# Sixteen experts of a mixture-of-experts layer taken two at a time, one in each 64-column half of TensorE

## The chip, the core and the metric

The kernel runs on one core of one Trainium2 chip. The metric is the device time of one execution in microseconds; lower is better. TensorE (PE) multiplies, ScalarE (ACT) and VectorE (DVE) empty the accumulation banks (PSUM) and do elementwise work, GpSimd (POOL) adds and broadcasts, and SyncE (SP) issues the transfers (DMA).

## What is computed

One decoder layer over 256 tokens of 2048 channels. A token-mixing part gives x1; each token is then routed to 2 of 16 experts. An expert has two input matrices of 2048 x 1024 (gate, up) and one output matrix of 1024 x 2048 (down):

```python
def expert_block(args):
    xb, e = args
    hb = jax.nn.silu(xb @ w_gate[e]) * (xb @ w_up[e])
    return hb @ w_down[e]
...
x = _layer_norm(ALPHA * x + mix, ln1_g[i], ln1_b[i])
...
ple = jax.nn.sigmoid(x @ ple_w_gate[i]) * (p[i] @ ple_w_proj[i])
x = _layer_norm(ALPHA * x + ffn + ple, ln2_g[i], ln2_b[i])
```

`ffn` is the sum over a token's two experts, weighted by the router. All is float32.

## The kernel before, in words

SBUF holds 12 large buffers of 16 KB per partition (`B`, `NB = 12`). Most of them hold weights: `load_one` (L129) takes one buffer for one load of 2 MB, `prefetch` (L142) starts loads as long as buffers are free beside those in `state["reserve"]`, and `done` (L152) gives a buffer back after its last matmul and calls `prefetch`. All loads go over SP's queue in one fixed order (`spec`), and each waits there until the readers of the buffer that it takes are done. `keep(n)` sets buffers aside; `BR` turns one of them into a long-lived tile.

**First part** (token mixing, L226 to L520): every weight piece is split into two rounded parts (float32r, `hi` and `lo`), and three float32r products replace one float32 product.

**Expert part.** For each expert `e`, `gate_up` takes 8 loads: 16 chunks of 128 channels times two matrices times two 512-column pieces. The tokens of the expert (up to 64 slots, `CAP`) are the 64-column stationary operand, and the two 512-column pieces of one matrix run in the two 64-column halves of the array (`mm_gu`, L755, matmul L757). `hidden` (L760) makes silu(gate) * up out of the two banks, turns it by four transposes (L775) and copies it to SBUF before the down product may begin. `mm_d` (L780, matmul L783) then takes 4 loads. The result is copied out by ACT (`evac`, L789), and `combine` (L812) brings the slots back to the tokens: a float32 product with the weighted selection matrix `PT`, in eight products of 64 rows (L801), with eight DVE additions into `acc` (L810). This runs as `late` work inside the next expert's `hidden`.

Small work is put between the loads by a list `bg`, from which `pop_bg` takes one piece after each load: `gather` (L702, matmuls L708), which builds the tokens `xg` of the next pair of experts by a one-hot product; `spread` and `weighted` (L678, L686: the weighted selection matrices, transposes L696); `keep_T` (transposes of x1 for the gated embedding) and `residual`.

After each of experts 6 to 13 comes one block of the gated embedding, `ple` (L728): 8 short matmuls (L737) and 64 long ones (L742) on one load. Its second weight, `wp`, lies in a large buffer of its own. Long-lived in large buffers are x1, xg, `misc` (the selection matrices and the copied results), acc, from expert 4 on x1T, and from expert 6 on wp.

Before the last expert stands `overflow` (L925): a branch that runs only if an expert has over 64 tokens, and that every engine must pass (L927). The last expert's columns come in blocks of 256, 256, 256, 128 and 128 (`last_expert`, L854), with statistics (L898) after each; then follow the layer norm (L1040, L1045) and the eight stores (L1059).

Of the kernel before, what the change touches and what calls it, by code (L numbers as in the profile page):

```python
# [17 lines left out]
T = 256  # L18
# [8 lines left out]
SCALE = 128.0 ** -0.5  # L27
NB = 12
PLE0 = 6
# [3 lines left out]
def trunk(ctx, tc, I, out):  # L33
# [69 lines left out]

    xw, xd = I["exp_w"], I["exp_d_last"]

    def spec_ple(i):
        spec(("ple", i), [(slice(0, 4096), I["ple_w_gate"][i].rearrange("p c f -> p (c f)"))])

    def spec_exp(e):
        for i in range(8):  # L110
            spec(("gu", e, i), [(slice(0, 4096), xw[e, i])])
        for i in range(4):
            spec(("ed", e, i), [(slice(0, 4096), xw[e, 8 + i] if e < NE - 1 else xd[i])])

    for e in range(NE):
        spec_exp(e)
        if e == PLE0 - 1:
            spec(("wp", 0), [(None, I["ple_w_proj"].rearrange("(c p) d -> p c d", p=128), 2)])
        if 0 <= e - PLE0 < 8:
            spec_ple(e - PLE0)  # L120
# [7 lines left out]

    def load_one():  # L129
        key, parts = loads[state["next"]]  # L130
        t = B("w")
        for p in parts:
            if p[0] is None:
                d = t if len(p) == 3 else t[:, p[3]:p[3] + 8 * p[4]]
                SP.dma_start(d.rearrange("p (c f) -> p c f", c=p[2]), p[1])
            else:
                SP.dma_start(t[:, p[0]], p[1])  # L137
        tiles[key] = t
        state["next"] += 1
        state["out"] = state.get("out", 0) + 1  # L140
# [71 lines left out]
    slots = C("slots", [128, 2, 64])  # L212
    POOL.iota(slots, pattern=[[0, 2], [1, 64]], base=1, channel_multiplier=0, allow_small_or_imprecise_dtypes=True)
# [452 lines left out]
    grp = {}  # L666
    back = {}
    long = {}

    def onehot(g):  # L670
        P = S("P")[:, 0:256].rearrange("p (a e s) -> p a e s", a=2, e=2)
        es = slice(2 * g, 2 * g + 2)
        for a in range(2):
            DVE.tensor_tensor(P[:, a], slots[:, 0:1, :].to_broadcast([128, 2, CAP]),  # L674
                              pos[:, a, es, None].to_broadcast([128, 2, CAP]), op=OP.is_equal)
        grp[g] = (P.rearrange("p a e s -> p a (e s)"), xgs[:, g % 2])

    def spread(e):  # L678
        W = S("W").rearrange("p (a e k s) -> p a e k s", a=2, e=2, k=2)
        for k in range(2):  # L680
            for a in range(2):
                DVE.tensor_scalar(W[:, a, k], slots, pos[:, a, e + k:e + k + 1], wA[:, a, e + k:e + k + 1],
                                  op0=OP.is_equal, op1=OP.mult)
        back[e] = W

    def weighted(e):  # L686
        if not long.get("misc"):
            long["misc"] = BR("misc").rearrange("p (i f) -> p i f", i=8)
            long["pT"] = long["misc"][:, 7, :].rearrange("p (c t) -> p c t", c=2)
            SP.dma_start(long["pT"], I["pT"])  # L690
        W = back[e]
        PT = long["misc"][:, (e // 2) % 2, :]
        ps = AUX()
        for k in range(2):
            for a in range(2):
                PE.transpose(ps[:, k * T + a * 128:k * T + (a + 1) * 128],  # L696
                             W[:, a, k].rearrange("p k s -> p (k s)"), ident)
        ACT.activation(PT, ps, AF.Copy)
        back[e] = PT[:, 0:T]
        back[e + 1] = PT[:, T:2 * T]  # L700

    def gather(g, cp):  # L702
        P, xg = grp[g]
        ps = AUX()
        for j in range(2):
            c = 2 * cp + j
            for a in range(2):
# [5 lines left out]
                          op0=OP.mult, op1=OP.add)  # L713

# [13 lines left out]
    def ple(i):  # L728
        if i == 0:
            long["wp"] = take(("wp", 0)).rearrange("p (c d) -> p c d", c=2)  # L730
# [4 lines left out]
        for a in range(2):  # L735
            for c in range(2):
                PE.matmul(pw[:, a * 256:(a + 1) * 256], long["pT"][:, c, a * 128:(a + 1) * 128], long["wp"][:, c, cs],  # L737
                          start=(c == 0), stop=(c == 1))
# [10 lines left out]
        POOL.tensor_add(long["acc"][:, :, cs], long["acc"][:, :, cs], s.rearrange("p (a f) -> p a f", a=2))  # L749
        done()  # L750
        if i == 7:
            free(2)
# [7 lines left out]
    def hidden(pg, pu, late=None, fill=0):  # L760
        s = S("s")
        hT = S("hT")
        ps = AUX()
        for k in range(2):
# [3 lines left out]
            DVE.tensor_mul(s[:, ks], s[:, ks], pu[:, ks])  # L768
        while late:
            late.popleft()()  # L770
        if fill:
            busy(fill)
# [5 lines left out]
        return hT.rearrange("p (j k s) -> p j k s", j=4, k=2)  # L778

    def mm_d(py, hT, w, fc):  # L780
        for b in range(2):
            for hf in range(2):
# [29 lines left out]
    def combine(y, PT, first=False):  # L812
        for b in range(2):
            for a in range(2):
                combine_unit(y, PT, first, a, b)
# [304 lines left out]
```

## Time and profile before

| | |
|---|---|
| time, median of 3 runs | 1643.28 us (1642.66 to 1643.73) |
| the profiled execution, its own time | 1642.69 us |
| its span, first to last instruction | 1641.0 us |
| PE busy | 1595.6 us (97%) |
| DVE busy | 559.9 us (34%) |
| ACT busy | 400.0 us (24%) |
| moved by DMA | 540.10 MB, mean 329 GB/s |

The first part takes about the first 615 us, the expert part the rest. "Busy" of PE counts pipelined matmuls with modelled ends, so that a nearly full share does not say that the array works at its peak. The GB/s of the DMA are read by stretch: the largest value that any long stretch shows is the measure of a full stretch.

### The profile page before, as it was taken

How to read it: one execution, taken by the hardware profiler on the slowest of the kernel's cores; microseconds unless marked ns; L12 is line 12 of the kernel's file. 1: busy time of each engine (PE TensorE's matmuls, PEld its weight loads, DVE VectorE, ACT ScalarE, POOL GpSimd, SP SyncE). 2: the span in 40 equal slices, each digit the busy share in tenths (PEclk: the TensorE clock that was granted, in tenths of full speed). 3: DMA queues.
4: the chain of work that ended last, by engine and by line, in shares of the span. 5: the costliest groups of instructions: out<-in, count | busy, mean ns of one | idle time of the engine just before them, and what ended most of it. 6: DMA issues, size and time to landing. Idle time of an engine off the chain costs nothing. (4 is left out here: it accounts for less than half of the span.)

```text
span 1641.0 us, 18130 instructions
## 1 busy us (share of the span) xinstructions
PE 1595.6 (97%) x7558; PEld 941.1 (57%) x7558; DVE 559.9 (34%) x996; ACT 400.0 (24%) x700; POOL 40.0 (2%) x41
## 2 busy tenths in 40 slices
PE   8999999999999999999999999999999999999994
PEld 6888878888888874433333344453544535445323
DVE  6555675656556652122022211112011120111126
ACT  5555555454545441100001000000000000000001
POOL 0000000000000000000000000000000000000012
PEclk9999999999999999999999999999999999999997
DMA  9743544255557767999999999999998999999994
GB/s 387 330 154 137 182 181 192 116 205 185 182 198 292 295 242 298 394 397 427 427 427 426 427 425 427 426 424 428 389 427 374 379 428 374 426 382 373 427 384 170
DMA packets 42586, 540.10 MB, mean 329 GB/s; under 512 B 7042, under 2 KB 7042, under 8 KB 9602
## 3 DMA queue, kind: packets, MB, share of 16 engines
q1 hardware_dynamic: 42500, 538.90, 80.3%
q8 instruction: 60, 0.98, 0.2%
q14 instruction: 26, 0.21, 0.0%
HBM read 536.78 MB, written 2.10 MB: 328 GB/s over the span
## 5 line engine op out<-in xcount | busy, mean ns | idle before, releaser
L757 PE MATMUL mm<-w,xg 128*64 128x512 f32 x2048 | 461.3, 598 | 4.4 <-PEq L927 2.6
L283 PE MATMUL mm<-pc,xh 128*128 128x512 f32 x1152 | 362.8, 395 | 6.0 <-ACT pc L264 5.4
L265 DVE TENSOR_TENSOR pc<-w,pc 128x512 fp32r<-128x512 f32 x416 | 290.9, 710 | 198.9 <-ACT pc L264 196.3
L264 ACT ACTIVATE pc<-w 128x512 fp32r<-128x512 f32 x416 | 259.7, 630 | 233.4 <-DVE pc L265 179.8
L757 PEld LDWEIGHTS mm<-w,xg 128*64 128x64 f32 x2048 | 139.7, 137 | 265.8 <-issue 249.7
L283 PEld LDWEIGHTS mm<-pc,xh 128*128 128x128 f32 x1152 | 213.8, 189 | 51.2 <-ACT pc L264 5.9
L283 PE MATMUL mm<-pc,xl 128*128 128x512 f32 x576 | 225.4, 391 | 0.0
L783 PE MATMUL mm<-w,hT 128*64 128x512 f32 x960 | 211.3, 595 | 0.0
L783 PEld LDWEIGHTS mm<-w,hT 128*64 128x64 f32 x960 | 66.8, 137 | 127.2 <-issue 126.6
L712 DVE TENSOR_SCALAR xg<-aux,gc 128x128 f32<-128x128 f32 x64 | 26.2, 410 | 318.2 <-ACT xg L711 318.2
L283 PEld LDWEIGHTS mm<-pc,xl 128*128 128x128 f32 x576 | 108.5, 188 | 22.9
L742 PE MATMUL mm<-w,x1T 128*128 128x256 f32 x512 | 111.8, 379 | 0.0
L742 PEld LDWEIGHTS mm<-w,x1T 128*128 128x128 f32 x512 | 97.3, 190 | 13.2
L711 ACT ACTIVATE xg<-aux,gc 128x128 f32<-128x128 f32 x64 | 29.3, 458 | 287.0 <-PE aux L708 287.0
L708 PEld LDWEIGHTS aux<-P,x 128*128 128x128 f32 x512 | 61.9, 191 | 51.0 <-issue 50.3
L748 DVE TENSOR_TENSOR s<-s,aux 128x512 f32<-128x512 f32 x8 | 5.5, 688 | 238.5 <-ACT s L747 238.5
L283 PE MATMUL mm<-pc,mixh 128*128 128x512 f32 x256 | 79.0, 390 | 0.0
L801 PE MATMUL aux<-misc 64*128 64x512 f32 x240 | 73.4, 629 | 2.6 <-DVE acc L810 2.6
L708 PE MATMUL aux<-P,x 128*128 128x128 f32 x512 | 73.8, 287 | 0.7 <-DVE P L674 0.7
L810 DVE TENSOR_TENSOR acc<-acc,aux 128x512 f32<-128x512 f32 x112 | 68.4, 680 | 14.8 <-PE aux L801 14.8
L767 DVE TENSOR_TENSOR s<-s,mm 128x256 f32<-128x256 f32 x32 | 13.4, 418 | 160.3 <-ACT s L766 160.3
L794 ACT ACTIVATE misc<-mm 128x512 f32<-128x512 f32 x30 | 17.7, 597 | 182.4 <-PE mm L783 182.4
(197 smaller groups left out, 834.1 us busy)
## 6 DMA issues: line engine op xcount, KB each, us to landing
w<-in_exp_w_dram SPq DMA_DIRECT2D x188, 2048.0 KB, 14.1
w<-in_w_in_dram SPq DMA_DIRECT2D x34, 2048.0 KB, 8.5
w<-in_w_o_dram SPq DMA_DIRECT2D x8, 2048.0 KB, 8.2
w<-in_ple_w_gate_dram SPq DMA_DIRECT2D x8, 2048.0 KB, 14.1
w<-in_w_out_a_dram SPq DMA_DIRECT2D x4, 2048.0 KB, 8.2
w<-in_w_out_b_dram SPq DMA_DIRECT2D x4, 2048.0 KB, 8.4
w<-in_exp_d_last_dram SPq DMA_DIRECT2D x4, 2048.0 KB, 30.8
w<-in_w_in_dram SPq DMA_DIRECT2D x3, 1024.0 KB, 12.7
```

What stands on the lines that cost most here:

```text
L264: ACT.activation(hi, w, AF.Copy)
L265: DVE.tensor_sub(lo, w, hi.bitcast(F32))
L283: PE.matmul(ps[a], l[:, c, as_], r, start=(first and n == 0), stop=(last and n == 2))
L708: PE.matmul(ps[:, j * 128:(j + 1) * 128], x1[:, a, c * 128:(c + 1) * 128], P[:, a, :], start=(a == 0), stop=(a == 1))
L711: ACT.activation(xg[:, c, :], ps[:, 0:128], AF.Identity, scale=gc[:, 0, c:c + 1], bias=gc[:, 1, c:c + 1])
L712: DVE.tensor_scalar(xg[:, c + 1, :], ps[:, 128:256], gc[:, 0, c + 1:c + 2], gc[:, 1, c + 1:c + 2], op0=OP.mult, op1=OP.add)
L742: PE.matmul(ps[:, a * 256:(a + 1) * 256], x1T[:, c, a * 128:(a + 1) * 128], w[:, c, :], start=(c == 0 and a == 0), stop=(c == DC - 1), ski ...
L757: PE.matmul(ps[64 * hf:64 * hf + 64, :], x, w[:, hf * 512:(hf + 1) * 512], start=(c == 0), stop=(c == DC - 1), skip_group_check=True, tile ...
L783: PE.matmul(py[b][64 * hf:64 * hf + 64, :], hT[:, fc % 4, fc // 4, :], w[:, hf * 1024 + b * 512:hf * 1024 + b * 512 + 512], start=(fc == 0 ...
L794: ACT.activation(y[-1], p, AF.Copy)
L801: PE.matmul(ps, PT[64 * hf:64 * hf + 64, a * 128:(a + 1) * 128], y[b][64 * hf:64 * hf + 64, :], start=True, stop=True, tile_position=(64 * ...
L810: DVE.tensor_add(xb, xb, pss[hf])
```

## The change

Experts are taken in pairs. For a pair `g`, one 64-column half of TensorE holds the tokens of one expert, the other half those of the other, and each of the four 512-column products of a chunk is now two matmuls, one per expert, into one bank. The work of a pair is four products of two banks each: "A" and "B" (each half of the hidden channels, gate and up, 8 loads) and "0" and "1" (each half of the output columns, 4 loads). The weights lie in DRAM in that order. The turn of a product's hidden rows is not done between the products but after the fourth chunk of the next product ("A") or the third of it ("B"). The routing weight is multiplied in on the hidden rows (`wc`), so that the selection matrix holds only 0 and 1 (`PO`); the results are split into two rounded parts and go back to the tokens by 128-row float32r products of both experts at once (`scatter`), one after each chunk of the following product. Small work is taken after each chunk, that is twice per load. `misc` and `wp` no longer take large buffers; the embedding blocks (`PLE`) stand in pairs 1 to 6, twice in pairs 4 and 5. The overflow branch stands before the last pair. The last pair's last 1024 columns come in blocks of 512, 256, 128 and 128.

```diff
-PLE0 = 6
+
+PLE = [(1, "B"), (2, "B"), (3, "B"), (4, "B"), (4, "1"), (5, "B"), (5, "1"), (6, "B")]
...
+    Pm = C("Pm", [128, 2, 2, 128])
+    PO = C("PO", [128, 2, T], F32R)
+    wc = C("wc", [128, NP + 1])
+    hTs = [C(f"hT{k}", [128, 4, 128]) for k in range(2)]
+    pT = C("pT", [128, 2, T])
+    SP.dma_start(pT, I["pT"])
...
+    def selection(P, w, i, n):
         ps = AUX()
...
+        for a in range(2):
+            PE.transpose(ps[:, a * 128:(a + 1) * 128], P[:, a], ident)
+        for a in range(2):
+            PE.matmul(ps[:, 256:258], P[:, a], w[:, a, :], start=(a == 0), stop=(a == 1), skip_group_check=True)
+        ACT.activation(PO[:, i, :], ps[:, 0:T], AF.Copy)
...
     def mm_gu(ps, x, w, c):
-        for hf in range(2):
-            PE.matmul(ps[64 * hf:64 * hf + 64, :], x, w[:, hf * 512:(hf + 1) * 512],
-                      start=(c == 0), stop=(c == DC - 1), skip_group_check=True, tile_position=(0, 64 * hf))
...
+        for k in range(2):
+            for e in range(2):
+                es = slice(64 * e, 64 * e + 64)
+                PE.matmul(ps[k][es, :], x[:, es], w[:, e, k, :], start=(c == 0), stop=(c == DC - 1),
+                          skip_group_check=True, tile_position=(0, 64 * e))
...
+    def inner(ph, g, xg, at):
+        ps = [MM(), MM()]
+        for i in range(8):
+            w = take((ph, g, i)).rearrange("p (c e k f) -> p c e k f", c=2, e=2, k=2)
+            for j in range(2):
+                mm_gu(ps, xg[:, 2 * i + j, :], w[:, j], 2 * i + j)
+                if j:
+                    done()
+                step(at, 2 * i + j)
+        return ps
...
+    def hidden(ps, n):
+        pg, pu = ps
         s = S("s")
...
+            DVE.scalar_tensor_tensor(s[:, ks], s[:, ks], wc[:, n:n + 1], pu[:, ks], op0=OP.mult, op1=OP.mult)
+        return s
...
+    def evac(ps, n=512):
         y = []
...
+        for p in ps:
+            h, l = S("yh", F32R)[:, 0:n], S("yl", F32R)[:, 0:n]
+            ACT.activation(h, p[:, 0:n], AF.Copy)
+            DVE.tensor_sub(l, p[:, 0:n], h.bitcast(F32))
+            y.append((h, l))
         return y
...
+    def scatter(y, i, o, a, first=False, n=512, stat=None):
+        ps = AUX()
+        for j in range(2):
+            PE.matmul(ps[:, 0:n], PO[:, i, a * 128:(a + 1) * 128], y[j], start=(j == 0), stop=(j == 1))
+        xb = long["acc"][:, a, o:o + n]
+        if first:
+            DVE.tensor_copy(xb, ps[:, 0:n])
...
+            DVE.tensor_add(xb, xb, ps[:, 0:n])
+        if stat is not None:
+            DVE.bn_stats(fst[:, a, stat, :], xb)
...
+    keep(2)
+    onehot(Pm[:, 0], pair_of(pos, 0))
+    gather(Pm[:, 0], xgs[:, 0], 0)
+    gather(Pm[:, 0], xgs[:, 0], 1)
     weights()
...
+        if g == NP - 1:
+            for f in back:
+                f()
+            back = []
+            keep(-2)
+            overflow()
+        ps = inner("A", g, xg, events(back, 1))
...
+        s = hidden(ps, g)
+        ples(g, "A")
+        ps = inner("B", g, xg, {3: lambda: turn_hidden(s, hTs[0])})
+        s = hidden(ps, g)
+        ples(g, "B")
+        if g == 0:
+            long["acc"] = BR("acc").rearrange("p (a d) -> p a d", a=2)
+        ps = outer("0", g, {2: lambda: turn_hidden(s, hTs[1])})
...
+        y = evac(ps)
+        ples(g, "0")
+        at = events(scatters(y, i, 0, g == 0, 0 if g == NP - 1 else None), 1)
...
+        ps = outer("1", g, at)
+        drain()
+        back = scatters(evac(ps), i, 1024, g == 0)
+        ples(g, "1")
```

How this moves the instructions, at three places. On PE, between the end of one expert's input product and its down product, followed by an embedding block, there stood before (L757 input products, L801 the way back to the tokens, L775 turn, L783 down, L737 and L742 embedding):

```order
L757 MATMUL mm<-w,xg 64x512 x24
L801 MATMUL aux<-misc 128x512 x8
L775 MATMUL aux<-ident,s 128x128 x4
L783 MATMUL mm<-w,hT 64x512 x32
L737 MATMUL aux<-w,misc 128x256 x4
L742 MATMUL mm<-w,x1T 128x256 x32
L757 MATMUL mm<-w,xg 64x512 x8
L708 MATMUL aux<-P,x_3542 128x128 x4
L757 MATMUL mm<-w,xg 64x512 x8
```

Now, for a pair, from the end of product "A" on (L746 input products, L799 turn, L723 and L728 embedding, L753 down, L816 the way back):

```order
L746 MATMUL mm<-w,xg 64x512 x24
L799 MATMUL aux<-ident,s 128x128 x4
L746 MATMUL mm<-w,xg 64x512 x48
L723 MATMUL aux<-wpt,pT 128x256 x4
L728 MATMUL mm<-w,x1T 128x256 x32
L753 MATMUL mm<-w,hT_4316 64x512 x12
L799 MATMUL aux<-ident,s 128x128 x4
L753 MATMUL mm<-w,hT_4316 64x512 x4
L753 MATMUL mm<-w,hT_4317 64x512 x16
L753 MATMUL mm<-w,hT_4316 64x512 x8
L816 MATMUL aux<-yh,PO 128x512
L816 MATMUL aux<-yl,PO 128x512
```

The turn stands three or four chunks into the following product, and the way back is a pair of 128-row products at a time between chunks of the next product, where before it was eight 64-row products in a row directly ahead of the turn.

On PE at the start of the expert part the first tokens are gathered. Before (L708 gather, one piece per load of eight matmuls):

```order
L757 MATMUL mm<-w,xg 64x512 x8
L708 MATMUL aux<-P,x_3542 128x128 x4
L757 MATMUL mm<-w,xg 64x512 x8
L708 MATMUL aux<-P,x_3542 128x128 x4
L757 MATMUL mm<-w,xg 64x512 x8
```

Now (L693 gather, two pieces per load):

```order
L693 MATMUL aux<-Pm,x_3543 128x128 x8
L746 MATMUL mm<-w,xg 64x512 x4
L693 MATMUL aux<-Pm,x_3543 128x128 x4
L746 MATMUL mm<-w,xg 64x512 x4
L693 MATMUL aux<-Pm,x_3543 128x128 x4
L746 MATMUL mm<-w,xg 64x512 x4
```

Each load of the first pair now has two pieces of small work on it, so that its buffer comes free later.

On SP around the overflow branch there stood before (the branch is L926 to L928; the loads after it come as the last rows of the queue):

```order
L1004 DMA rows<-in_ln_g_dram 1x2048
L1005 DMA rows<-in_ln_b_dram 1x2048
L137 DMA w<-in_exp_w_dram 128x4096 x12
L926 TENSOR_LOAD cmi
L926 ISA x2
L927 COMPARE_AND_BRANCH
```

Now:

```order
L131 DMA w<-in_ple_w_gate_dram 128x4096
L133 DMA wpt<-in_ple_w_proj_dram 128x512
L131 DMA w<-in_exp_w_dram 128x4096 x14
L864 TENSOR_LOAD cmi
L864 ISA x2
L865 COMPARE_AND_BRANCH
```

After the branch 7 loads were left before (3 of the last expert's input weights, 4 of its output weights); now 18 are left, 10 and 8. The embedding's second weight comes as eight small loads (256 KB, `wpt`), each behind its first.

## Rows read from the trace of the kernel before

**Rows 1.** The page, busy tenths in 40 slices of the span (41 us each).

```profile
PE   8999999999999999999999999999999999999994
PEclk9999999999999999999999999999999999999997
GB/s 387 330 154 137 182 181 192 116 205 185 182 198 292 295 242 298 394 397 427 427 427 426 427 425 427 426 424 428 389 427 374 379 428 374 426 382 373 427 384 170
```

**Rows 2.** Busy time by stretch: engine busy us (instructions), granted clock, DMA share, GB/s.

```profile
core 0: us, PE busy (x) PEld busy (x) DVE busy (x) ACT busy (x) POOL busy (x), PEclk, DMA share, GB/s
560.00:600.00 40.00, 40.00 (x178) 33.10 (x178) 25.29 (x39) 18.77 (x30) 0.00 (x0) 1.00 0.57 210
620.00:632.00 12.00, 11.35 (x66) 5.76 (x65) 6.46 (x33) 1.37 (x3) 0.00 (x0) 1.00 0.14 32
632.00:680.00 48.00, 47.54 (x242) 19.88 (x240) 5.70 (x15) 5.40 (x12) 0.00 (x0) 1.00 0.98 391
720.00:730.00 10.00, 9.54 (x45) 3.23 (x45) 2.96 (x7) 0.37 (x1) 0.00 (x0) 1.00 0.79 301
730.00:1010.00 280.00, 273.56 (x1302) 104.55 (x1300) 54.56 (x113) 26.10 (x55) 0.00 (x0) 1.00 1.01 427
1104.00:1520.00 416.00, 413.06 (x1930) 200.19 (x1928) 60.84 (x124) 30.37 (x63) 7.64 (x6) 1.00 0.95 398
1230.00:1242.00 12.00, 12.00 (x57) 7.66 (x57) 2.19 (x3) 0.60 (x1) 1.28 (x1) 1.00 0.64 246
1562.00:1566.00 4.00, 4.00 (x12) 1.56 (x14) 2.61 (x4) 0.00 (x0) 2.02 (x1) 0.58 1.01 424
1572.00:1580.00 8.00, 8.00 (x36) 2.28 (x34) 2.57 (x4) 0.00 (x0) 0.00 (x0) 1.00 0.59 199
1600.00:1612.00 12.00, 10.75 (x100) 6.77 (x98) 3.66 (x11) 0.95 (x2) 0.00 (x0) 1.00 0.96 405
620.00:1614.00 994.00, 976.32 (x4645) 432.04 (x4644) 171.71 (x378) 80.68 (x170) 14.67 (x10) 1.00 0.96 404
```

**Rows 3.** Waits of SP's queue: who waited for whom, us in total, times, longest us.

```profile
SPq L137 <- PE mm L757: 436.2, 111, 21.3
SPq L137 <- PE mm L783: 281.2, 58, 13.4
SPq L927 <- SPq L927: 21.0, 3, 11.2
```

**Rows 4.** Waits of PE from 640 to 1540 us, longest first, complete.

```profile
PE aux L775 <- ACT hT L777: 6.7, 14, 0.5
PE aux L801 <- DVE acc L810: 2.6, 2, 1.4
PE mm L757 <- DMA w<-in_exp_w_dram: 1.6, 2, 1.2
```

**Rows 5.** PE in order of time: start us, us, instruction, count [idle before].

```profile
629.30 1.16 PE L708 MATMUL aux<-P,x 128*128 128x128 f32 x8
630.39 3.65 PE L757 MATMUL mm<-w,xg 128*64 128x512 f32 x16
633.97 1.16 PE L708 MATMUL aux<-P,x 128*128 128x128 f32 x8
...
1495.98 1.99 PE L737 MATMUL aux<-w,misc 128*128 128x256 f32 x8
1497.81 13.98 PE L742 MATMUL mm<-w,x1T 128*128 128x256 f32 x64
1511.72 27.69 PE L757 MATMUL mm<-w,xg 128*64 128x512 f32 x128
1539.34 4.89 PE L801 MATMUL aux<-misc 64*128 64x512 f32 x16
1544.16 0.44 PE L775 MATMUL aux<-ident,s 128*128 128x128 f32 x2
...
1545.43 13.95 PE L783 MATMUL mm<-w,hT 128*64 128x512 f32 x64
```

**Rows 6.** The chain that ended last, from 1570 us: start us, us, what.

```profile
1577.92 30.76 DMA w<-in_exp_d_last_dram
```

**Rows 7.** PE and DVE in order of time behind the last load.

```profile
1613.62 1.97 PE L866 MATMUL mm<-w,hT 128*64 128x128 f32 x32 [0.55 <-DMA w<-in_exp_d_last_dram]
...
1620.26 0.47 DVE L895 TENSOR_TENSOR acc<-acc,aux 128x128 f32<-128x128 f32 x2
...
1621.82 0.69 DVE L1028 BATCH_NORM_AGGREGATE fmv<-fst 128x2 f32<-128x60 f32 x2
```

**Rows 8.** Groups of ACT and DVE, 640 to 1600 us: busy us, mean ns of one.

```profile
L794 ACT ACTIVATE misc<-mm 128x512 f32<-128x512 f32 x30 | 17.7, 597 | 182.4 <-PE mm L783 182.4
L810 DVE TENSOR_TENSOR acc<-acc,aux 128x512 f32<-128x512 f32 x112 | 68.4, 680 | 14.8 <-PE aux L801 14.8
```

More of the change, by code (lines that the diff above doesn't have):

```diff
@@ L686, in weighted @@
[L686 to L692, printed above, removed]
-        ps = AUX()
[L694 to L700, printed above, removed]
@@ L713, in gather, with pair_of @@
                           op0=OP.mult, op1=OP.add)
+    def pair_of(t, g):
+        return t[:, :, 2 * g:2 * g + 2]
     def keep_T(pr):
@@ L767, in hidden, with turn_hidden @@
             DVE.tensor_mul(s[:, ks], s[:, ks], pg[:, ks])
[L768 to L772, printed above, removed]
+            DVE.scalar_tensor_tensor(s[:, ks], s[:, ks], wc[:, n:n + 1], pu[:, ks], op0=OP.mult, op1=OP.mult)
+        return s
+    def turn_hidden(s, hT):
+        ps = AUX()
+        hT = hT.rearrange("p j s -> p (j s)")
         for k in range(2):
@@ L787, in trunk @@
-    turn = [0]
-    def evac(py):
-        y = []
-        for p in py:
-            y.append(long["misc"][:, 3 + turn[0] % 4, :])
-            turn[0] += 1
-            ACT.activation(y[-1], p, AF.Copy)
-        return y
-    def combine_unit(y, PT, first, a, b):
-        pss = []
-        for hf in range(2):
-            ps = AUX()
-            PE.matmul(ps, PT[64 * hf:64 * hf + 64, a * 128:(a + 1) * 128],
-                      y[b][64 * hf:64 * hf + 64, :], start=True, stop=True, tile_position=(64 * hf, 0))
-            pss.append(ps)
-        for hf in range(2):
-            o = hf * 1024 + b * 512
-            xb = long["acc"][:, a, o:o + 512]
-            if first:
-                DVE.tensor_copy(xb, pss[hf])
-            else:
-                DVE.tensor_add(xb, xb, pss[hf])
@@ L812, in combine @@
[L812 to L815, printed above, removed]
-    def gate_up(e, xg):
-        pg, pu = MM(), MM()
-        for i in range(8):
-            w = take(("gu", e, i)).rearrange("p (k c f) -> p k c f", k=2, c=2)
-            for k, ps in enumerate((pg, pu)):
-                for j in range(2):
-                    mm_gu(ps, xg[:, 2 * i + j, :], w[:, k, j, :], 2 * i + j)
-            done()
-            pop_bg()
-        if e == 0:
-            return hidden(pg, pu, fill=6)
-        return hidden(pg, pu, late)
@@ L974, in overflow @@
-                    combine(evac(py), PT)
-                free()
-    fst = C("fst", [128, 2, 10, 6])
-    fmv = C("fmv", [128, 2, 2])
-    frs = C("frs", [128, 2, 2])
-    onehot(0)
-    gather(0, 0)
-    gather(0, 1)
+                    DVE.tensor_scalar(ce[:, 0], ce[:, 0], -float(CAP), None, op0=OP.add)
+                    P = Pm[:, 0]
+                    onehot(P, ce[:, 0])
+                    selection(P, ce[:, 1], 0, NP)
+                    for cp in range(8):
+                        gather(P, xg, cp)
```

355 lines of the change are left out of this document (139 added, 216 removed).

## The prediction

> **What bounds the kernel now.** Read first the slices of the page [rows 1]. PE is busy in every slice, and the GB/s tell two parts apart: up to about 615 us the transfers run at a third to two thirds of what they can, and PE sets the time; the change touches nothing there that lies on PE's path. From slice 17 on the transfers stand at 427 GB/s in most slices while PE is still full, so this part has two candidates. The stretches [rows 2] give the measure: 280 us at 427 GB/s (730 to 1010) is a full stretch. A load of 2.097 MB then takes 2.097/0.427 = 4.91 us.
>
> Which of the two leads is read from the waits. SP waits for PE's last matmul on a buffer before nearly every load, 169 times and 717 us in all [rows 3]; PE waits for a load only twice between 640 and 1540 us, for 1.6 us in all [rows 4]. So PE leads, and the transfers are only just full enough to keep up. Over the whole part, 620 to 1614 us, they move 404 GB/s [rows 2], which leaves 994 x (1 - 404/427) = 53.5 us in which the queue had nothing to do. Those microseconds are what a lighter PE can win, and no more: the last thing that PE waits for is the last load [rows 6, 7].
>
> Where the 53.5 us lie [rows 2]: 620 to 632, all ten free buffers full and none released: 12 x (1 - 32/427) = 11.1. 632 to 680, `misc` and acc take buffers: 48 x (1 - 391/427) = 4.0. 720 to 730: 3.0. 1104 to 1520, 416 x (1 - 398/427) = 28.3, in six notches like the one at 1230 to 1242 (5.1), each behind an embedding block of 15.7 us (1495.98 to 1511.72 [rows 5]) that releases one buffer at its end while only six buffers hold weights. 1572 to 1580, behind the overflow branch, where SP waited for landings [rows 3]: 4.3. The end: 0.6. Together 51.3; I use this.
>
> **What the change does to PE.** Prices from [rows 5]: eight loads of input products without small work take 1539.34 - 1511.72 = 27.62, or 3.45 us per load; a down load 13.95/4 = 3.49. A gather piece takes 630.39 - 629.30 = 1.09, and the load behind it 633.97 - 630.39 = 3.58, so that an interruption costs 0.13 more.
>
> Taken away per pair of experts: two combines of 4.82 us (1539.34 to 1544.16), two turns that stop PE for 1.27 (1544.16 to 1545.43), the turn of the weighted matrices. Added: 16 float32r matmuls of 128 x 512. In the first part 178 matmuls, nearly all of this kind, fill 40 us [rows 2], 0.225 each, so 3.6 us. Two turns without a stop, 0.5 each; the selection, 0.7. The count of products on weights stays: 24 loads. Sum of a pair: 24 x 3.45 = 82.8; eight gathers 8.7; 3.6 + 1.0 + 0.7; some 19 interruptions at 0.13 = 2.5. About 99.5 us, against 24 x 4.91 = 117.8 us of transfer. An embedding block adds 15.7 to PE and 4.91 + 0.6 (its small second load at the same rate) to the queue: a pair with one stands at 115 against 123, one with two (pairs 4, 5) at 131 against 129. So the queue leads nearly everywhere, and PE arrives early.
>
> Can the queue run dry all the same? Behind an embedding block only if PE holds all buffers. Eight buffers now hold weights from the second pair on (x1, xg, acc, x1T take four), not six. PE's lead of landed loads is four or five after the first pair and shrinks by about 18 us per pair less 10 per embedding block; with two or three landed, the queue has four or more loads outstanding, 20 us, against 15.7. No notches are left: 28.3 us go. The 4.0 and the 3.0 near the start go too, but others come in their place.
>
> **What remains or comes.** (a) The wait at 620 to 632: 11.1, and the first release is one gather later, 1.1: 12.2. (b) The first pair gathers twice per load, so releases come every 3.45 + 2 x 1.22 = 5.9 us, less where the selection stands; six such spacings lose about 4 against 4.91. (c) x1T takes a buffer in product "B" of the first pair; the next load waits for two releases, 5.9 and 4.7 (two pieces of four transposes, 0.5 each, in place of the gathers), less 4.91: 5.7. I take 5, because the releases just before are a little early. acc takes its buffer some 30 us later, when the queue is some 5 us ahead: 0. (d) The branch: SP waits again until all outstanding loads have landed, now with 18 loads to go instead of 7, but it loses one start-up either way: 4.3. PE's own stop there (it goes on at 1562, after the down product that began at 1545.43 and ran 13.95 [rows 5]) is hidden under six landed loads. Sum 25.5, against 51.3: -25.8. The input pT (0.3 MB, 0.6 us) now loads inside wait (a): -0.6.
>
> **The end.** From PE's start on the last load to the end of statistics the kernel needs 1621.82 - 1613.62 = 8.2 us [rows 7], with DVE doing four additions and four statistics for each of two blocks. Now there are two of each per block (128 channels x 128 rows instead of two 64-row halves): product 1.9, way back of the block before 0.5, product 1.9, ACT and DVE split 0.6, product 0.3, two additions and two statistics at some 0.2 each 0.8: 6.0. That is -2. The layer norm and stores stay.
>
> **ACT and DVE** get four more copies and subtractions per pair at 0.6 and 0.7 us and lose eight additions of 0.68 [rows 8]; both are idle two thirds of the time, which hides it.
>
> **Sum.** -25.8 - 0.6 - 2 = -28.4. The profiled execution took 1642.69 us on its own clock (span 1641.0), 0.6 below the median of the runs shown; I predict 1642.7 - 28.4 = 1614.3, say **1614 us**. By itself the forecast runs from 1603 ((b) to (d) hidden by earlier releases, -11) to 1624 (10 us of notches left in pairs 4 and 5).
>
> **Rivals.** *PE still leads.* The spare time is small: 8 x 99.5, plus 8 x 15.7 for the embedding, plus some 15 for x1T and residual, less 9 for the gathers that the last pair has not, is 928 us, and the branch 6; the queue's own time from 632 to the last landing near 1588 is 956. That leaves 22 us, or 0.11 us per load. If a load costs 3.75 instead of 3.45 + 0.1 (interruptions twice as often), PE needs 40 us more, 18 of them visible: 1632. Chance 0.10. For it: PE has never yet been asked to change between 64-column halves and full width so often. The Trainium skill, "TensorEngine Tiling (Array Packing)", section "Key Properties", says that changing the tiling mode drains the array; the 0.13 of [rows 5] is the price of such a change here, two crossings together, and agrees with a small drain.
>
> *The way back waits (slower).* Each scatter needs ACT's copy (0.6) and DVE's subtraction (0.7) of its rows and a free bank; if the two engines come late, PE, which works in order, stops in the middle of the next product with all its loads behind it. 64 scatters: at 1.3 us each, the longer of the two seen for a combine being 1.4 [rows 4], PE loses 83 us, 61 beyond its spare: 1614 + 61 = 1675. It turns slower from 0.8 us per scatter (51 = 22 + 28). Against it: the first scatter stands two chunks (3.5 us) behind the product's end, and 1.3 to 2.7 us suffice for both parts of both banks. Chance 0.06.
>
> *The clock.* PE now waits for loads, and its clock may fall. After the stop at the branch the granted clock was 0.58 from 1562 to 1566 [rows 2], the lower level, 1.2 GHz, for most of it. In 1600 to 1612 [rows 2] PE waited for its loads too (0.55 before the last [rows 7]) and the clock stayed at 1.00. The waits now expected are up to 4.91 - 3.45 = 1.5 us per load. If the clock fell to 1.2 GHz in half of all loads and a load then took 6.9, PE would need 96 x 3.45 = 331 us more, far beyond its spare, 1614 + 309 = 1923; but a PE at half clock has no wait left and would be busy without a gap, the state in which every full slice shows clock 9 [rows 1]. Chance 0.03. The Trainium skill, "TensorE: Matmul & The Clock Gate", section "HAM oscillation — how this bites in real kernels", shows a kernel whose clock fell in each wait for a load; the row at 1600 speaks for shorter waits being harmless, and no row here has waits in between.
>
> *No change.* The queue is slowed elsewhere (the branch holds SP for several loads, acc's buffer comes late) and gives the gain back: 1640 to 1646. Chance 0.05.
>
> **How the numbers follow.** Forecast 0.76, PE still leads 0.10, no change 0.05, slower 0.09. Measurement tells about 0.2% (3.3 us) from no change. Faster: 0.76 + 0.10 = 0.86; same 0.05; slower 0.09. The range takes the forecast's own from 1603 and the first rival up to 1636.
>
> **What would show it.** Right: the stretches after the first pair stand at 427 GB/s through all embedding blocks, PE has many waits for w, SP waits less for PE, last load landing near 1588. Wrong: PE again without waits for loads and the GB/s below 427 (PE leads); waits of L816 for ACT or DVE; granted clock under 1 between 640 and 1550; a dip at the branch of over 5 us.

## The result and the profile after

The changed kernel takes **1623.59 us** (median of 4 runs, 1622.63 to 1624.73) against 1642.97 us for the kernel before, run beside it (4 runs, 1642.5 to 1643.73): ratio 0.9882, 95% interval 0.9865 to 0.9899, a gain of 19.4 us. The forecast was 1614 with a range from 1603 to 1636.

The slices of the page after (40 of 40.5 us each; engine rows in tenths busy, then the granted clock and the rate of transfers):

```profile
span 1621.5 us, 17768 instructions
PE   8999999999999999999999999999999999998984
PEclk9999999999999999999999999999999999999997
GB/s 387 338 156 116 188 203 154 158 173 191 207 172 263 347 182 282 325 414 427 427 427 428 427 428 427 427 427 428 428 425 427 428 427 427 408 423 414 391 428 167
```

Against [rows 1] the notches behind the embedding blocks are gone: from slice 18 to slice 33 the row of transfers reads 425 to 428 throughout. What is left lies at the start (slices 16 and 17) and around the overflow branch (34 to 37). The stretches give it in microseconds (columns as in [rows 2]):

```profile
620.00:632.00 12.00, 11.34 (x67) 6.21 (x65) 5.55 (x30) 1.60 (x4) 0.00 (x0) 1.00 0.08 29
632.00:680.00 48.00, 48.00 (x257) 22.51 (x258) 8.66 (x25) 8.51 (x19) 0.00 (x0) 1.00 0.87 323
680.00:720.00 40.00, 39.08 (x186) 13.52 (x184) 6.34 (x13) 4.90 (x10) 0.00 (x0) 1.00 0.99 406
720.00:1400.00 680.00, 673.84 (x3153) 302.80 (x3150) 105.93 (x204) 52.46 (x111) 8.88 (x7) 1.00 1.01 427
1400.00:1480.00 80.00, 79.02 (x372) 36.01 (x372) 9.25 (x20) 5.84 (x13) 5.75 (x3) 1.00 0.99 414
1480.00:1515.00 35.00, 28.67 (x120) 10.37 (x118) 5.17 (x9) 1.20 (x2) 0.00 (x0) 0.90 0.90 372
```

With the prediction's own measure, length x (1 - rate/427), the empty time of the queue is:

| stretch | forecast | measured |
|---|---|---|
| 620 to 632, term (a) | 12.2 | 12 x (1 - 29/427) = 11.2 |
| 632 to 720, terms (b) and (c) | 4 + 5 = 9 | 11.7 + 2.0 = 13.7 |
| 720 to 1400, embedding blocks | 0 | 0 |
| 1400 to 1480 | 0 | 80 x (1 - 414/427) = 2.4 |
| the branch, term (d) | 4.3 | 35 x (1 - 372/427) = 4.5 |
| sum (before: 51.3) | 25.5 | 31.8 |

So the queue lost 51.3 - 31.8 = 19.5 us of emptiness. PE starts on the last load at 1594.12 where it was 1613.62 [rows 7], also 19.5, and the time fell by 19.4: the gain is the queue's, to within 0.1 us. Both kernels move the same amount (540.10 and 540.09 MB) and both end behind their last load, so these figures have to agree; that they do doesn't say what made the loads come earlier, which is what the experiments are for.

But the queue does not lead alone. The waits after, PE's and then SP's (us in total, times, longest), stand here; L746 are the products on input weights, L753 those on output weights, L816 the way back, L799 the turns, L865 the branch:

```profile
PE aux L799 <- ACT hT L801: 7.8, 16, 0.5
PE mm L746 <- PEq L865: 6.2, 1, 6.2
PE mm L753 <- DMA w<-in_exp_d_last_dram: 5.1, 4, 1.3
...
PE aux L723 <- DMA wpt<-in_ple_w_proj_dram: 1.3, 1, 1.3
PE mm L746 <- DMA w<-in_exp_w_dram: 1.1, 1, 1.1
```

```profile
SPq L131 <- PE mm L746: 485.5, 116, 22.1
SPq L131 <- PE mm L753: 199.2, 53, 8.1
```

PE waited once for a load of input weights, 1.1 us, and four times for the last pair's output weights, and SP still waits for PE before nearly every load (169 times and 685 us, against 169 times and 717 us in [rows 3]). From 720 to 1400 both are full: the transfers at 427 GB/s, and PE with hardly a wait. The two look tied, which the experiments test.

Where PE's forecast surplus went is seen in its order of time (start us, us, instruction, count):

```profile
727.73 1.03 PE L753 MATMUL mm<-w,hT 128*64 128x512 f32 x4
728.69 0.50 PE L816 MATMUL aux<-yh,PO 128*128 128x512 f32 x1
729.03 0.39 PE L816 MATMUL aux<-yl,PO 128*128 128x512 f32 x1
729.35 1.94 PE L753 MATMUL mm<-w,hT 128*64 128x512 f32 x8
731.22 0.50 PE L816 MATMUL aux<-yh,PO 128*128 128x512 f32 x1
...
1490.56 0.39 PE L816 MATMUL aux<-yh,PO 128*128 128x512 f32 x1
1490.78 0.40 PE L816 MATMUL aux<-yl,PO 128*128 128x512 f32 x1
1491.02 0.40 PE L816 MATMUL aux<-yh,PO 128*128 128x512 f32 x1
```

A rounded matmul alone between 64-column ones takes 0.34 and 0.32 us from start to start (728.69, 729.03, 729.35); in a row of its own kind, just ahead of the branch, 0.22 to 0.24. The eight matmuls behind a product take 731.22 - 729.35 = 1.87, against 1.73 undisturbed (a quarter of the 6.92 us in which 32 of them run in the ninth experiment). One product of the way back costs 0.34 + 0.32 + 0.14 = 0.80 us, where 0.45 + 0.13 = 0.58 had been forecast. And the turns stop PE as before: 16 times, 7.8 us in all, where "no stop" was forecast.

### The profile page after: what moved, and what is told of

Same layout as the page of the kernel before. It is cut to its first block, busy times and chain, and to the rows that moved or that the text cites. A ratio compares the mean times of both kernels' runs of the same rounds, so it can differ in the third digit from the quotient of the medians.

```text
span 1621.5 us, 17768 instructions
## 1 busy us (share of the span) xinstructions
PE 1571.2 (97%) x7386; PEld 925.9 (57%) x7386; DVE 539.9 (33%) x926; ACT 398.1 (25%) x698; POOL 39.9 (2%) x41
## 2 busy tenths in 40 slices
DMA packets 43465, 540.09 MB, mean 333 GB/s; under 512 B 7154, under 2 KB 7154, under 8 KB 10738
## 5 line engine op out<-in xcount | busy, mean ns | idle before, releaser
L746 PE MATMUL mm<-w,xg 128*64 128x512 f32 x2048 | 469.1, 600 | 7.3 <-PEq L865 6.2
L746 PEld LDWEIGHTS mm<-w,xg 128*64 128x64 f32 x2048 | 137.5, 137 | 252.4 <-issue 230.7
L753 PE MATMUL mm<-w,hT 128*64 128x512 f32 (+2 forms) x1088 | 231.4, 572 | 5.2 <-DMA w<-in_exp_d_last_dram 5.1
L753 PEld LDWEIGHTS mm<-w,hT 128*64 128x64 f32 x1088 | 73.0, 136 | 138.6 <-issue 131.6
L728 PE MATMUL mm<-w,x1T 128*128 128x256 f32 x512 | 111.8, 379 | 0.0
L728 PEld LDWEIGHTS mm<-w,x1T 128*128 128x128 f32 x512 | 97.3, 190 | 13.2
L693 PEld LDWEIGHTS aux<-Pm,x 128*128 128x128 f32 x512 | 61.9, 191 | 51.0 <-DVE xg L697 30.8
L693 PE MATMUL aux<-Pm,x 128*128 128x128 f32 x512 | 73.8, 287 | 0.7 <-DVE Pm L672 0.7
L821 DVE TENSOR_TENSOR acc<-acc,aux 128x512 f32<-128x512 f32 (+2 forms) x60 | 38.8, 651 | 94.5 <-PE aux L816 94.5
L807 ACT ACTIVATE yh<-mm 128x512 fp32r<-128x512 f32 (+2 forms) x34 | 19.5, 573 | 200.9 <-PE mm L753 200.9
L789 ACT ACTIVATE s<-mm 128x256 f32<-128x256 f32 x32 | 12.3, 384 | 217.2 <-PE mm L746 207.7
L808 DVE TENSOR_TENSOR yl<-mm,yh 128x512 fp32r<-128x512 f32 (+2 forms) x34 | 22.4, 659 | 101.4 <-ACT yh L807 101.4
```

Of the source, the lines that this page charges most:

```text
L693: PE.matmul(ps[:, j * 128:(j + 1) * 128], x1[:, a, c * 128:(c + 1) * 128], P[:, a, :], start=(a == 0), stop=(a == 1))
L728: PE.matmul(ps[:, a * 256:(a + 1) * 256], x1T[:, c, a * 128:(a + 1) * 128], w[:, c, :], start=(c == 0 and a == 0), stop=(c == DC - 1), ski ...
L746: PE.matmul(ps[k][es, :], x[:, es], w[:, e, k, :], start=(c == 0), stop=(c == DC - 1), skip_group_check=True, tile_position=(0, 64 * e))
L753: PE.matmul(p[es, 0:n], hTs[fc // 4][:, fc % 4, es], w[:, e, b * n:(b + 1) * n], start=(fc == 0), stop=(fc == 7), skip_group_check=True, t ...
L807: ACT.activation(h, p[:, 0:n], AF.Copy)
L808: DVE.tensor_sub(l, p[:, 0:n], h.bitcast(F32))
```

## The experiments

Three readings stand against each other. P and Q were there from the first run on; T came out of runs 5 to 8, and runs 9 to 11 test it. **T (tied):** from 720 to 1400 the load queue and PE need the same time, so lightening one of them alone gains little, burdening one of them costs nearly in full, and only moving both gains. **P:** PE alone sets the pace, so each microsecond of PE counts both ways. **Q:** the queue alone sets it, so PE's work is free within its surplus. All ratios are to the kernel before, run beside. Differences in us are between medians of separate sittings, in which the kernel before took 1642.97 to 1643.56 us, so that less than about 1 us says little.

**1. Way back without its low half** (PE lighter by one matmul in each of its products).

```diff
-            h, l = S("yh", F32R)[:, 0:n], S("yl", F32R)[:, 0:n]
+            h = S("yh", F32R)[:, 0:n]
...
-            DVE.tensor_sub(l, p[:, 0:n], h.bitcast(F32))
...
-        for j in range(2):
-            PE.matmul(ps[:, 0:n], PO[...], y[j], start=(j == 0), stop=(j == 1))
+        PE.matmul(ps[:, 0:n], PO[...], y[0], start=True, stop=True)
```

> The changed kernel without the low half of the results: 64 subtractions on VectorE and 68 float32r matmuls on TensorE are left out (the tokens get rows rounded once). In the changed kernel a scatter takes 0.81 us of TensorE, half of it for the low part: about 64 x 0.34 = 22 us less work for TensorE, 3 us per pair. Theory Q (the queue of loads sets the end, TensorE only has to keep up): 427 GB/s stays from 720 us on, only the dip at 1410 us (1.8 us) can go: 1620 to 1624, -0 to -3. Theory P (TensorE sets the pace, and the queue is full only because it is as fast): most of the 22 us show: 1602 to 1608. In both TensorE's waits for loads grow.

Measured: 1620.98 us (1620.61 to 1621.37), ratio 0.9864 (0.9849 to 0.9879), 2.6 us below the change and inside Q's 1620 to 1624. The saving is smaller than the expectation's 22 us. In order of time, and then PE's waits:

```profile
729.09 0.49 PE L814 MATMUL aux<-yh,PO 128*128 128x512 f32 x1
731.38 0.50 PE L814 MATMUL aux<-yh,PO 128*128 128x512 f32 x1
```

```profile
PE mm L746 <- DMA w<-in_exp_w_dram: 9.8, 8, 1.2
...
PE mm L753 <- DMA w<-in_exp_d_last_dram: 6.0, 6, 1.3
...
PE aux L723 <- DMA wpt<-in_ple_w_proj_dram: 3.3, 2, 1.9
```

A step with a way back takes 731.38 - 729.09 = 2.29 us, where it took 731.22 - 728.69 = 2.53 with both halves: 0.24 for each of some 60, or about 14 us (an estimate from these rows). Of these, 11.6 came back as waits for loads (19.1 us in these three rows instead of 7.5), and 2.6 show in the time. Little else moved: PE starts on the last load at 1593.73 instead of 1594.12, because what the dip at 1400 to 1480 gave back (423 GB/s instead of 414) went at the branch (383 GB/s from 1480 to 1530 instead of 390). The end without the low half is shorter by 1.6 us (statistics at 1600.41, 6.68 behind that start). A lighter PE alone has nothing to win before the end: P, as far as it says that less work of PE shows, falls.

**2. Six buffers for weights in pairs 1 to 5**, as the kernel before had: two buffers are held by an idle tile.

```diff
-    keep(2)
+    keep(4)
...
+        if g == 1:
+            keep(-2)
+            idle = [B("idle") for _ in range(2)]
+            for t in idle:
+                DVE.memset(t[:, 0:1], 0.0)
```

> The changed kernel with two buffers held idle in pairs 1 to 5, so that six hold weights there as in the kernel before, not eight. Theory Q with both parts needed (lighter TensorE and more buffers): the notches behind the embedding blocks return in pairs 1 to 5 (seven blocks, 2 to 5 us each): +10 to +28 us, 1634 to 1652, GB/s below 427 behind each block. Theory that the lighter TensorE alone made the gain: no change, 1622 to 1626.

Measured: 1631.61 us (1631.03 to 1634.04), ratio 0.9932 (0.9918 to 0.9945): 8.0 us above the change, between the two expectations (1634 to 1652, 1622 to 1626). Part of the empty time is back, but mostly not where it was expected:

```profile
720.00:1400.00 680.00, 670.36 (x3114) 301.69 (x3112) 104.74 (x206) 51.47 (x109) 8.88 (x7) 0.99 1.00 419
720.00:780.00 60.00, 60.00 (x288) 23.63 (x286) 12.31 (x26) 6.43 (x13) 0.00 (x0) 1.00 0.98 389
1230.00:1290.00 60.00, 60.00 (x293) 31.45 (x293) 10.24 (x21) 5.40 (x12) 1.27 (x1) 1.00 0.98 395
```

The first embedding block (L728) starts only at 812.33, so the 60 x (1 - 389/427) = 5.3 us before 780 stand ahead of all of them. They and most of the 4.5 us from 1230 to 1290 fall where a gather stands on every chunk (753.62, 756.58, 759.53 and so on), which frees a buffer every 2 x 2.96 = 5.9 us. Of the seven embedding blocks in pairs 1 to 5, only the second ones of pairs 4 and 5 (at 1230.38 and 1364.73) have a dip behind them; behind the other five the rate stays at 426 to 428 GB/s with six buffers too. So most of the notches of [rows 2] are gone without the two buffers; by these rows the buffers serve above all to carry the queue over the stretches with gathers. The change also spreads the blocks (one each in pairs 1, 2, 3 and 6, where eight experts in a row had one each); what that is worth alone wasn't tried.

**3. The kernel before with a seventh buffer**: its second embedding weight comes in small loads as in the change (with the setting `dynamic_dma_scratch_size=1024`, which the change has too); nothing else is taken over.

```diff
-            spec(("wp", 0), [(None, I["ple_w_proj"].rearrange("(c p) d -> p c d", p=128), 2)])
...
+    wpt = C("wpt", [128, 2, 2, 256])
...
+        if key[0] == "ple":
+            SP.dma_start(wpt[:, key[1] % 2], I["ple_w_proj"][key[1]])
```

> The kernel before with the second weight of the embedding in small loads, as the change has it, so that its large buffer holds weights: seven instead of six from expert 6 on, TensorE's work as before. If buffers alone made the gain, the notches of 28 us shrink and the time falls by 8 to 20 us, to 1623 to 1635. If TensorE's lighter work made it, the notches shrink but the time stays, because TensorE hardly ever waited for a load there: 1639 to 1643.

Measured: 1639.16 us (1637.51 to 1642.62), ratio 0.9979 (0.9969 to 0.9988): 4 us. From 1104 to 1520 the rate went from 398 to 402 GB/s alone. One buffer more from expert 6 on, without a lighter PE, gains little; two more weren't tried on the kernel before. A lighter PE without its two buffers (run 2) keeps 11 of its 19 us.

**4. Without the overflow branch** (left out; with these inputs no expert overflows).

```diff
             keep(-2)
-            overflow()
```

> The changed kernel without the overflow branch (it would not handle an expert with over 64 tokens; there is none here). Theory Q: the queue gains the 4.3 us in which it stood empty at 1490 to 1510: 1618 to 1621, -3 to -6. Theory P: TensorE gains its stop of 6.2 us and the start at the low clock, 1.8: 1615 to 1617, and loads wait more.

Measured: 1620.0 us (1619.38 to 1620.62), ratio 0.9857 (0.9842 to 0.9873): 3.6 us below the change. The stretch from 1480 to 1515 then stands at 428 GB/s instead of 372. Term (d) was 4.3. This is inside Q's range; PE's own stop of 6.2 us goes in this run too, and does not show.

**5. The start alone** (`e5_start`): small work of the first pair runs at every second step once its own tokens are gathered, and the turns into `x1T` wait for the second pair.

```diff
-        else:
+        elif n % 2 or not calm[0]:
             pop_bg()
...
-        if g == 0:
+        if g == 1:
+            calm[0] = False
             bg.extend([lambda pr=pr: keep_T(pr) for pr in range(8)])
```

> The changed kernel with the first pair's small work spread: once its own tokens are gathered, one piece per load instead of two, and the turns of x1 (which take a large buffer) in the second pair, not the first. TensorE's work is the same. Theory Q: from 632 to 720 us the queue stands empty for 13.7 us in the changed kernel; a release every 4.7 us instead of 5.9 keeps it nearly full, some 4 us remain, and the buffer of x1T is taken when loads are queued: 1613 to 1617, -7 to -10. Theory P: no change, 1622 to 1625, because TensorE does the same work.

Measured: 1621.34 us (1621.08 to 1622.43), ratio 0.987 (0.9855 to 0.9885): only 2.3 us, outside both ranges. The queue did win its start, but lost it again where it had been full:

```profile
632.00:680.00 48.00, 47.54 (x244) 20.29 (x243) 6.97 (x19) 5.92 (x14) 0.00 (x0) 1.00 0.98 396
680.00:720.00 40.00, 39.54 (x194) 14.77 (x193) 5.06 (x12) 4.09 (x9) 0.00 (x0) 1.00 1.01 428
720.00:1400.00 680.00, 675.10 (x3166) 304.36 (x3166) 109.15 (x211) 56.05 (x118) 8.87 (x7) 1.00 1.00 423
```

At the start 13.7 us of emptiness became 48 x (1 - 396/427) = 3.5; from 720 to 1400 there are now 680 x (1 - 423/427) = 6.4, and from 1400 to 1480, at 401 GB/s, 4.9 instead of 2.4. PE waits for expert inputs for 0.3 us in all: PE sets the pace there. This miss is what brought reading T in place of Q.

**6. PE heavier**: 14 more bfloat16 matmuls of 128 x 512 behind the first down product of each of seven pairs (3.13 us each in the trace, 22 in all); the output does not use them.

```diff
         y = evac(ps)
+        if g < NP - 1:
+            busy(14)
```

> The changed kernel with 14 idle matmuls (128 x 512, bfloat16) more in each of the first seven pairs: 3.0 us of TensorE each, 21 in all. Theory Q: TensorE holds some five landed loads and three are on the way (13 us) around 1400 us, so that about half of the 21 us is taken up by the buffers and the rest shows: +5 to +13 us, 1629 to 1637. Theory P: all shows, +19 to +23, 1643 to 1647.

Measured: 1641.72 us (1641.36 to 1642.5), ratio 0.9992 (0.9983 to 1.0001): 18.1 us above the change, most of what was added and between the two expectations (+5 to +13, +19 to +23), with the transfers from 720 to 1400 down to 419 GB/s. With run 1: some 14 us less of PE gain 2.6, some 22 us more cost 18. The change stands at the corner that T says.

**7. The way back as one plain float32 product** of one copy.

```diff
-    PO = C("PO", [128, 2, T], F32R)
+    PO = C("PO", [128, 2, T])
...
-            h, l = S("yh", F32R)[:, 0:n], S("yl", F32R)[:, 0:n]
+            h = S("yh")[:, 0:n]
```

> The changed kernel with the way back as one float32 product of 128 rows instead of two rounded ones: no split on VectorE (64 subtractions fewer). In the trace of before a plain float32 product of 64 columns costs 2 x 0.22 us, of 128 columns twice that, so a scatter should take 0.86 to 1.0 us of TensorE against 0.81: 3 to 12 us more work in all. Theory Q: within the buffers, 1622 to 1627, no change. Theory that the rounded products are what made the gain: +8 or more, over 1631.

Measured: 1641.61 us (1640.93 to 1642.98), ratio 0.9991 (0.9982 to 1.0). PE in order of time:

```profile
726.54 1.12 PE L814 MATMUL aux<-yh,PO 128*128 128x512 f32 x2
727.60 1.94 PE L753 MATMUL mm<-w,hT 128*64 128x512 f32 x8
```

The two passes take 727.60 - 726.54 = 1.06 us, where the rounded pair takes 0.66. Times some 60 products that is 24 us of PE, of which 18.0 show. So the reading that the rounded products made the gain came true (over 1631), and Q's 1622 to 1627 did not. Pairs of experts and eight buffers without the rounding give nothing. This doesn't make the rounding special: run 6 shows that any other 22 us of PE cost as much. It is needed because it is the part that makes PE lighter by that much.

**8. Run 5 with a shorter end**: the last two blocks of 128 columns go back by one plain float32 product.

```diff
+            if n == 128:
+                h = S("yh")[:, 0:n]
+                ACT.activation(h, p[:, 0:n], AF.Copy)
+                y.append((h,))
+                continue
...
```

> The start of e5_start, and the last two blocks of 128 columns go back by one plain float32 product each, so that TensorE no longer waits 1.1 us for VectorE's subtraction at the very end. Theory Q: e5_start's time less 0.5 to 1.5 us: 1612 to 1616.

Measured: 1620.96 us (1620.65 to 1621.17), ratio 0.9865 (0.985 to 0.988), 0.4 us below run 5, whose range it overlaps: not told apart from nothing, and outside the 1612 to 1616, which took run 5's own miss over.

**9. PE lighter with all of its work.** T now says that both limits have to be moved, and runs 5 and 7 say where. Here PE alone:

```diff
     def turn_hidden(s, hT):
-        for k in range(2):
-            for j in range(2 * k, 2 * k + 2):
-                PE.transpose(ps[:, j * 128:(j + 1) * 128], s[:, j * 128:(j + 1) * 128], ident)
+        for j in range(4):
+            PE.transpose(ps[:, j * 128:(j + 1) * 128], s[:, j * 128:(j + 1) * 128], ident)
+        for k in range(2):
...
     def events(fs, n0):
-        return {n0 + n: f for n, f in enumerate(fs)}
+        return {n0 + 2: lambda: [f() for f in fs]} if fs else {}
```

> The changed kernel with all of its work, made lighter on TensorE at the two prices that the trace shows: the four turns of a half stand together ahead of the two copies (the stop of 0.46 us in each of the 16 turns goes, about 7 us), and the four rounded products of a way back stand in one row at the third chunk (back to back a matmul is 0.235 us where alone between 64-column matmuls it is 0.335 us, and the longer chunk behind it comes once instead of four times: about 0.25 us for each of 60, some 15 us). So TensorE loses about 22 us, as in the run without the low half. Theory T (TensorE and the load queue are tied, the queue has 720 to 1400 full): like that run, 1620 to 1622 us, the queue at 427 GB/s from 720 to 1430, the last load landing at 1592 to 1594. Rival P (TensorE alone sets the pace): 1600 to 1605 us. Rival V (four products in one row wait for VectorE's adds, all four small banks are taken): TensorE waits about 1 us in each row, 15 us that eat the gain: 1623 to 1626 us.

Measured: 1621.6 us (1621.31 to 1622.08), ratio 0.9866 (0.9851 to 0.9881), as T said (Q would say the same of this run, P is out). Both prices went: no turn waits any more, and four products of a way back with their crossing take 730.71 - 728.65 = 2.06 us instead of 4 x 0.66, with one longer chunk behind them in place of four. PE's order of time, and then its longest wait in total:

```profile
728.65 0.50 PE L816 MATMUL aux<-yh,PO 128*128 128x512 f32 x1
728.99 0.39 PE L816 MATMUL aux<-yl,PO 128*128 128x512 f32 x1
729.22 0.40 PE L816 MATMUL aux<-yh,PO 128*128 128x512 f32 x1
...
730.39 0.39 PE L816 MATMUL aux<-yl,PO 128*128 128x512 f32 x1
730.71 7.09 PE L753 MATMUL mm<-w,hT 128*64 128x512 f32 x32
737.63 3.60 PE L746 MATMUL mm<-w,xg 128*64 128x512 f32 x16
```

```profile
PE mm L746 <- DMA w<-in_exp_w_dram: 17.0, 14, 2.8
```

The saving stands there as waits for loads, 17.0 us instead of 1.1. From 720 on the queue leads alone now.

**10. Both**: run 9 with the start of run 5 (the two diffs together).

> The run before with the start of the fifth experiment too: both of the things that are tied are moved, TensorE by about 22 us and the queue's start by about 9 us. Theory T: the dips that TensorE's pace left in 720 to 1460 with that start (some 7 us) go, the queue keeps its 9 us: last landing at 1582 to 1586, time 1611 to 1615 us. Rival Q (bandwidth at the end of the queue is all there is, what is gained at the start is lost later anyway): 1619 to 1622 us. Rival P: 1600 to 1605 us.

Measured: **1613.13 us** (1612.63 to 1613.92), ratio 0.9814 (0.98 to 0.9827), inside T's 1611 to 1615 and outside Q's and P's. The queue kept what it won:

```profile
632.00:680.00 48.00, 48.00 (x250) 21.02 (x246) 6.97 (x19) 5.81 (x14) 0.00 (x0) 1.00 0.98 396
680.00:720.00 40.00, 40.00 (x195) 14.81 (x196) 5.07 (x12) 4.09 (x9) 0.00 (x0) 1.00 1.01 427
720.00:1400.00 680.00, 674.18 (x3224) 316.46 (x3222) 108.81 (x219) 58.11 (x123) 8.88 (x7) 1.00 1.01 427
```

Two edits that gave 2.3 and 2.0 us alone give 10.5 together. PE starts to wait again, 10.5 us in 9 waits for the experts' input weights, so the queue leads now, and the branch takes more of it than before: 35 x (1 - 340/427) = 7.1 us from 1480 to 1515.

**11. Run 10 with the end of run 8.**

> The run before with the last two blocks of 128 columns sent back by one float32 product of one ScalarE copy. Both theories of the pace give the same as the run before less 0.3 to 1 us (0.4 was measured with TensorE's pace unchanged; where the last load lands earlier, the work behind it counts in full): 1610 to 1615 us by theory T, 1618 to 1621 us by rival Q.

Measured: 1612.67 us (1611.54 to 1613.1), ratio 0.9809 (0.9796 to 0.9822), inside T's range and the fastest version; its 0.5 us below run 10 lie within the overlap of their ranges.

## Why the prediction was right, and where not

*What could be won was right.* It was the empty time of the queue, and that is what the change won: 19.5 us there, 19.4 in the time. The largest term, the 28.3 us of notches behind the embedding blocks, went up to 1400 us. Runs 6 and 7 show that PE's lighter work, through the rounded way back, is needed for it: both have the eight buffers and the blocks as in the change, and neither gains anything. The two buffers, which the prediction gave as the reason, matter less: with six of them (run 2) five of seven blocks leave no notch. How much of it the spreading of the blocks does stays open.

*That the queue would lead, with PE 22 us ahead, was wrong*, as the steps below show; a last landing near 1588 did not come either, for PE starts on the last load at 1594.12. The measured 1623.6 us lie inside the forecast's own 1603 to 1624, but that is luck: its upper end stood for 10 us of notches left in pairs 4 and 5, and the time was lost elsewhere.

*The start* cost 13.7 us where (b) and (c) had 9. (b) itself was right: SP issued its loads at 631.03, 636.95, 642.86, 648.39, 653.06, 658.98 and 664.89, six spacings that lose 33.86 - 6 x 4.91 = 4.4 us, against 4. In (c) the gap where `x1T` takes its buffer was 676.33 - 664.89 = 11.4, a loss of 6.5: the step "I take 5, because the releases just before are a little early" failed, since the sum without it was 5.7. What the prediction had no term for is the rest, some 2.8 us: another spacing of 5.6 (681.24 to 686.83), and transfers that had loads outstanding and yet stood at 360 and 385 GB/s from 694 to 702, while each load landed 9 to 10 us after its issue. That so few outstanding loads don't fill the queue is what these rows suggest; it wasn't tried by itself.

*"Two turns without a stop"* failed. The copy of the first two transposes still stands between them and the next two (16 waits, 7.8 us); run 9, with four transposes ahead of the copies, has no such wait. That the common bank is the cause, and not the order of issue that the program gives, is argued and wasn't tried.

*"An interruption costs 0.13 more"* was carried from gathers to the way back, where an interruption costs 0.80 - 0.45 = 0.35. The rule that the prediction weighed ("TensorEngine Tiling (Array Packing)" of the Trainium skill, section "Key Properties": changing the tiling mode drains the array) agrees in direction; whether the time goes into a drain or into loading the other stationary operand, no run here tells apart. The price of such a change is not one number, but 0.13 around a gather and 0.35 around a rounded product.

Together these two make a pair 8 x 0.22 + 2 x 0.5 = 2.8 us longer, 22 us over eight pairs: all of the 22 us that the prediction gave PE as spare. So *"PE has many waits for w" failed*, and the first rival, PE still leading, was half right: not 18 us above the forecast, but a tie, which shows as the 2.4 us at 1400 to 1480 (0.7 are left in run 1, none in run 9) and as the corner of runs 1 and 6. Of these 2.4, 1.8 lie from 1410 to 1420 (351 GB/s), where the layer norm's parameters (`rows`) take a large buffer and SP waits 3.9 us for PE; the prediction had no term for that buffer.

*The end, -2 us,* did not come. From PE's start on the last load to the statistics it was 1602.37 - 1594.12 = 8.25 us against 8.2. In order of time on DVE:

```profile
1599.58 0.29 DVE L821 TENSOR_TENSOR acc<-acc,aux 128x128 f32<-128x128 f32 x1 [0.64 <-PE aux L816]
...
1600.12 0.27 DVE L821 TENSOR_TENSOR acc<-acc,aux 128x128 f32<-128x128 f32 x1
...
1600.63 0.27 DVE L808 TENSOR_TENSOR yl<-mm,yh 128x128 fp32r<-128x128 f32 x1
1601.32 0.29 DVE L821 TENSOR_TENSOR acc<-acc,aux 128x128 f32<-128x128 f32 x1 [0.42 <-PE aux L816]
...
1602.37 0.47 DVE L969 BATCH_NORM_AGGREGATE fmv<-fst 128x2 f32<-128x36 f32 x2
```

The prediction counted 0.2 us each for two additions and two statistics and let the split of the last block run beside them. It stands behind the four of the block before in DVE's order, and each costs about 0.27: on PE 1600.96 - 1599.11 = 1.85 us pass from the end of the last product to the low half of its result, where 0.6 were counted. Most of the rest is the way back of the block before, 1597.21 - 1596.02 = 1.19 against 0.5.

The three misses, 4.7 us at the start, 2 at the end and 2.4 at 1400, less 1.0 that term (a) came out better, are 8.1 of the 9.0 us between the forecast gain of 28.4 and the measured one. *The branch* was right (4.3 against 4.5; 3.6 of it is to be had, by run 4), *ACT and DVE* had room, and of the other rivals none came: PE waited for the way back only at the end, 1.3 us in two waits, and in the change the clock stayed at 1.00 from 632 to 1585 outside the branch.

## What to carry to other kernels

When two resources are both full over the same stretch, the change that frees one of them shows nearly nothing, and a test of one alone says that neither matters; try the two edits together before dropping either (2.0 and 2.3 us alone, 10.5 together). A forecast that hands an engine spare time should price each kind of interruption from a row of that kind, since 0.2 us on 64 of them was most of the spare here. Work of another shape between an engine's main products took less of the engine in one row than spread over the steps (run 9).

## What the runs showed of the hardware

The waits that a lighter PE gets can reach its clock. Run 10, PE in order of time, and the granted clock in two stretches behind it (columns as in [rows 2]):

```profile
1529.47 3.65 PE L746 MATMUL mm<-w,xg 128*64 128x512 f32 x16 [1.25 <-DMA w<-in_exp_w_dram]
1535.28 8.78 PE L746 MATMUL mm<-w,xg 128*64 128x512 f32 x32 [2.15 <-DMA w<-in_exp_w_dram]
```

```profile
1531.00:1535.00 4.00, 2.13 (x10) 0.43 (x6) 0.00 (x0) 0.00 (x0) 0.00 (x0) 1.00 0.99 422
1537.00:1539.00 2.00, 2.00 (x8) 0.61 (x6) 0.00 (x0) 0.00 (x0) 0.00 (x0) 0.50 0.98 418
```

Behind the wait of 1.25 us the clock stayed at 1.00; behind the one of 2.15 it stood at 0.50, the lower level of 1.2 GHz, for some 3.4 us (0.77, 0.50 and 0.88 in the three stretches of 2 us from 1535), and was back at 1.00 from 1541. It cost nothing that shows: the two loads then took 8.78 us of the 9.8 that the queue needs for two, and PE waited 1.00 us for the next.

The length of the wait alone doesn't decide it. Run 9 has a longer one, and the clock stayed:

```profile
1538.89 3.65 PE L746 MATMUL mm<-w,xg 128*64 128x512 f32 x16 [2.79 <-DMA w<-in_exp_w_dram]
```

```profile
1540.00:1542.00 2.00, 2.00 (x12) 0.57 (x8) 0.00 (x0) 0.00 (x0) 0.00 (x0) 1.00 1.02 434
```

In the same run the clock fell to 0.50 behind a wait of 2.01 us (before 1048.20) and stayed at 1.00 behind one of 2.02 (before 1172.46). So "shorter waits are harmless" held for the waits of up to 1.34 us that stand before most loads at the end of runs 9 and 10. The fall that the Trainium skill tells of in each wait for a load ("TensorE: Matmul & The Clock Gate", section "HAM oscillation — how this bites in real kernels") came here behind some waits of 2 us and more and not behind others; what tells them apart stays open.
